# A hybrid trunk kernel whose planner ranks instructions by deadlines and has other durations for some forms

## The chip, the cores and the metric

The kernel runs on one core of a Trainium2 chip. Its time is the device time in microseconds (us). Five instruction streams run side by side: TensorE (PE, matmuls), VectorE (DVE), ScalarE (ACT), GpSimd (POOL) and SyncE (SP, which here only issues DMAs). Each works its own instructions in a fixed order, and waits on semaphores for what another has not yet done.

## What is computed

Two layers of a trunk with three parallel token mixers, on 640 tokens (128 of context and 512 latent ones) of width 1024. All is float32. Cut to its core, one layer is:

```python
shift, scale, gate = split(mod, 3)          # mod = silu(c) @ w_mod + b_mod
h = rms(x, norm_g) * (1 + scale) + shift
proj = h @ w_in                             # all inputs of the branches and gates
o_a = attend(q, k, v)                       # latent attention, softmax over 640 keys
qkv = silu(dwconv(qkv_b, conv_w))           # gated DeltaNet, both directions, 4 heads
Tinv = triangular_solve(A + eye, eye)       # one 64x64 inverse per chunk, head, direction
o_b = rms(o_f + o_bw, gdn_onorm)
o_c = chunk_mlp(cu, cv)                     # gMLP with a 128x128 mixing matrix per group
yb = [o_a * silu(z_a), o_b * silu(z_b), o_c * silu(z_c)] @ w_branch
x = x + gate * (sum(sigmoid(gl) * yb) @ w_o)
```

## The kernel before

Tokens lie along the free dimension in two halves of 320, channels along the 128 partitions. A dense product of one 128-column block with 1024 input rows is three float32r products for each of eight row tiles (`mm3`: high by high, high by low, low by high), 128x320 each, into one PSUM bank; ACT casts a weight tile `raw` to its high part `hi`, and DVE subtracts that to get `lo`. `hh0` to `hh7` and `hl0` to `hl7` are the high and low parts of h.

The order of a layer in the program: modulation and norm, the four DeltaNet heads with the blocks for q, k and v, the chunk MLP and its blocks, the attention with the branches' products and gates in between, the merge, the output product. The inverse of a head (`inverse`, line 1066) goes in small steps between engines: DVE makes 16x16 inverses, PE multiplies 32x32 blocks (`pa`, line 1107; each step 20 matmuls with a `tile_position`, that is on a part of the array), ACT or DVE takes the result out of PSUM, and so on to 64x64. Its tiles are called `iv`, in PSUM `p2`.

Nothing of this is issued where it is written. `Recorder` records every operation with what it reads and writes; `issue` at the end emits them engine by engine, so that all instructions of the trace have the line 371. The order comes from `plan` (line 214): it simulates the five engines with the durations of `cost` (line 155), and each time an engine is free it takes, of the operations whose inputs and buffers are there, the one with the smallest `op.prio`. That number is the operation's place in the program, lowered by an offset (`rec.hp()`, 100000) for operations that free PSUM or feed the next step. Buffers are handed out in the order of the program for each kind (13 of `G`, 8 of `iv`, 5 of `C`, 3 each of `raw`, `hi` and `lo`, two PSUM banks each for the dense `dn`, for `mm` and for `p2`). `best` (line 206) plans once for each of four values of `SLACKS`, time that is added where PE waits for another engine, and keeps the order with the smallest modelled end.

Names of tiles carry two numbers, `iv_728_796`; below the second is left out. In the inverse of the third head, `R_727` is `brs` (lines 1100 to 1102), `iv_728` is `Bm` (lines 1103 to 1105), and `p2_729` is `pa`, the 20 matmuls that read it.

Of the kernel before, what the change touches and what calls it, by code (L numbers as in the profile page):

```python
# [8 lines left out]
F32R = mybir.dt.float32r  # L9
# [39 lines left out]
HOP = {"V": 36, "S": 36, "G": 60, "PE": 53, "SP": 60}  # L49
AFTER = {"V": 33, "S": 122, "G": 60}  # L50
SLACKS = (0, 60, 120, 180)
ISSUE = 475
DMA_LAG, DMA_RATE = 1900, 340.0

# [5 lines left out]
class Recorder:  # L60
# [94 lines left out]
    def cost(self, op, outs, ins):  # L155
        size = lambda x: x.free_size() if callable(x.free_size) else x.free_size
        e = op.eng
        op.ld = 0
        if e == "SP":
            big = max((x.nbytes() if callable(x.nbytes) else x.nbytes) for x in outs + ins)  # L160
            op.occ, op.lat = ISSUE, big / DMA_RATE
        elif e == "PE":
            n = size(outs[0])
            rows, cols = ins[0].ap[0][1], size(ins[0])
            if op.meth == "transpose":
                op.ld, op.occ = 109, n / 2.4 + 2
            elif ins[0].dtype == F32R:
                op.ld, op.occ = 109, n / 2.4 + 13.7
            elif rows <= 32:
                op.ld, op.occ = 15, n  # L170
            elif rows <= 64:
                op.ld, op.occ = 60, 2 * n
            elif cols == 32:
                op.ld, op.occ = 50, 0.43 * n
            elif cols == 64:
                op.ld, op.occ = 80, 1.3 * n
            else:
                op.ld, op.occ = 109, max(4 * n / 2.4 + 6, 222)
            op.lat = op.occ + 180
        else:  # L180
            n = max(size(x) for x in outs[:1] + ins[:1])
            ps = any(self.tag.get(x.tensor.name, ("", False, 0))[1] for x in outs + ins)
            if e == "V":
                quick = op.meth in ("tensor_scalar", "tensor_copy", "memset") and not ps
                d = 165 if n <= 16 else 165 + (0.66 if quick else 1.09) * n
                if n >= 250:
                    d = 150 + (0.63 if quick else 1.145 if n >= 640 and op.meth == "scalar_tensor_tensor" else 1.05) * n
                elif ps and n > 100:
                    d += 40
                if op.meth == "reciprocal":  # L190
                    d = 165 + 5.5 * n
            elif e == "S":
                d = 160 + 0.84 * n + (190 if "accum_out" in op.kw else 0)
                if op.meth == "activation" and n <= 128:
                    d = max(d, 350) + (45 if outs[0].dtype == F32R else 0)
                elif not ps or outs[0].dtype == F32R:
                    d += 45 if n <= 128 or op.meth == "activation" else 25 if n == 640 else 0
                if op.meth == "copy" and not ps and n == 512:
                    d = 620
            else:  # L200
                d = 200 + 1.2 * n
            op.occ, op.lat = d - TAIL[e], d
            if e == "S" and n == 160 and outs[0].ap[0][1] == 32:
                op.occ, op.lat = 260, 320

    def best(self):

        plans = []
        for slack in SLACKS:
            self.plan(slack)  # L210
            plans.append((self.total, slack))
        return self.plan(min(plans)[1])

    def plan(self, slack):
        import heapq
# [1594 lines left out]
```

## Time and profile before

| | |
|---|---|
| median of 3 runs | 1681.33 us (1680.39 to 1683.24) |
| the profiled execution, its own time | 1683.82 us |
| its span, first to last instruction | 1681.9 us |
| PE busy | 1636.5 us, 97% |
| DVE busy | 1284.8 us, 76% |
| ACT busy | 890.2 us, 53% |
| POOL busy | 16.7 us, 1% |
| mean granted clock of PE | 0.989 |

The span is that of one execution under the profiler; 1.9 us of its time lie outside it. Since PE is busy nearly throughout, the time is read as PE's work plus PE's waits: a list of waits says what PE waited for, and a timeline where. DVE and ACT count where PE waits for one of them. Stretches of 40 us show in which part of the program the waits lie: 0 to 60 us is the start, 120 to 320 the DeltaNet heads with the chunk MLP, 320 to 640 the attention, and the second layer repeats it 835 us later.

### The profile page before, as it was taken

The numbers are of one execution on the slowest core, as the hardware profiler recorded it, in microseconds if no ns is written. First come the engines' busy times: TensorE is split into PE (matmuls) and PEld (weight loads), VectorE is DVE, ScalarE is ACT, GpSimd is POOL, SyncE is SP. The second block draws the span as 40 slices with busy tenths as digits, with TensorE's granted clock in tenths as the row PEclk, the third lists the DMA queues.
The fourth block names the chain that finished last, engine by engine and source line by source line (L and its number), as shares of the span: only waits on it lengthen the run. The fifth ranks groups of instructions, "written<-read, shape, count | busy, mean of one in ns | idle before, by whom it ended". The sixth has DMA issues, their size and how long they took to land. (4 is left out here: it accounts for less than half of the span.)

```text
span 1681.9 us, 34993 instructions
## 1 busy us (share of the span) xinstructions
PE 1636.5 (97%) x13286; PEld 1538.7 (91%) x13286; DVE 1284.8 (76%) x3638; ACT 890.2 (53%) x2201; POOL 16.7 (1%) x100
## 2 busy tenths in 40 slices
PE   6999998999999999999999999989999999999998
PEld 5998988999889989989989989989998899899998
DVE  4898898665655768877988987976656557789898
ACT  3566664554545554434445676646545455545453
POOL 0000000000000000000000000000000000000000
PEclk9999999999999999999989999999999999999999
DMA  9312211222121212555542212212211122113342
GB/s 298 95 56 55 62 58 50 66 69 62 46 60 58 91 51 97 178 185 157 188 156 64 58 42 63 58 50 78 70 52 53 49 64 88 57 65 98 94 161 80
DMA packets 94616, 146.39 MB, mean 87 GB/s; under 512 B 14064, under 2 KB 38000, under 8 KB 94448
## 3 DMA queue, kind: packets, MB, share of 16 engines
q1 hardware_dynamic: 94448, 144.15, 28.0%
q8 instruction: 105, 1.72, 0.4%
q14 instruction: 63, 0.52, 0.1%
HBM read 132.28 MB, written 11.83 MB: 86 GB/s over the span
## 5 line engine op out<-in xcount | busy, mean ns | idle before, releaser
L371 PE MATMUL dn<-hh,hi 128*128 128x320 f32 (+1 forms) x1472 | 469.6, 319 | 4.8 <-ACT hh L371 2.1
L371 PE MATMUL dn<-hl,hi 128*128 128x320 f32 (+1 forms) x1472 | 469.1, 319 | 0.4 <-DVE hl L371 0.3
L371 PE MATMUL dn<-hh,lo 128*128 128x320 f32 (+1 forms) x1472 | 467.9, 318 | 0.0
L371 ACT CAST hi<-raw 128x512 fp32r<-128x512 f32 (+1 forms) x300 | 186.1, 620 | 198.5 <-PE dn L371 101.1
L371 PEld LDWEIGHTS dn<-hh,hi 128*128 128x128 f32 (+1 forms) x1472 | 277.1, 188 | 10.1 <-ACT hh L371 3.1
L371 PEld LDWEIGHTS dn<-hl,hi 128*128 128x128 f32 (+1 forms) x1472 | 277.6, 189 | 3.7 <-DVE hl L371 1.2
L371 PEld LDWEIGHTS dn<-hh,lo 128*128 128x128 f32 (+1 forms) x1472 | 277.5, 189 | 2.9 <-issue 1.0
L371 DVE TENSOR_TENSOR lo<-raw,hi 128x512 fp32r<-128x512 f32 (+1 forms) x300 | 206.5, 689 | 60.3 <-ACT hi L371 57.5
L371 PE MATMUL dn<-qkv,hi 128*128 128x320 f32 x768 | 175.0, 313 | 0.5 <-DVE iv L371 0.5
L371 PEld LDWEIGHTS dn<-qkv,hi 128*128 128x128 f32 x768 | 129.4, 189 | 3.3 <-ACT hi L371 1.6
L371 PE MATMUL dn<-qkv,lo 128*128 128x320 f32 x384 | 119.9, 312 | 0.0
L371 ACT CAST hi<-D 128x512 fp32r<-128x512 f32 x88 | 54.6, 623 | 105.9 <-PE dn L371 51.8
L371 PE MATMUL p<-hh,hi 128*128 128x320 f32 x296 | 92.3, 313 | 0.3 <-ACT hi L371 0.3
L371 PE MATMUL p<-hh,lo 128*128 128x320 f32 x296 | 92.2, 312 | 0.0
L371 PE MATMUL p<-hl,hi 128*128 128x320 f32 x296 | 92.0, 311 | 0.2 <-DVE hl L371 0.2
L371 DVE TENSOR_REDUCE mx<-p 128x1 f32<-128x640 f32 x64 | 52.7, 823 | 48.1 <-PE p L371 48.0
L371 ACT ACTIVATE V<-p,mx,scl 128x640 f32<-128x640 f32 x64 | 56.9, 888 | 60.5 <-DVE mx L371 57.2
L371 PEld LDWEIGHTS dn<-qkv,lo 128*128 128x128 f32 x384 | 72.4, 189 | 0.7 <-issue 0.7
L371 PE MATMUL p<-G,hi 128*128 128x320 f32 x286 | 69.3, 308 | 0.0
L371 ACT ACTIVATE th<-dn 128x320 f32<-128x320 f32 x112 | 48.7, 435 | 38.9 <-PE dn L371 38.2
L371 PEld LDWEIGHTS p<-iv,G 32*32 32x32 f32 (+2 forms) x608 | 34.9, 132 | 36.2 <-issue 33.1
L371 PE MATMUL p<-G,G 128*128 128x512 f32 x128 | 65.7, 595 | 0.0
(350 smaller groups left out, 3484.0 us busy)
## 6 DMA issues: line engine op xcount, KB each, us to landing
raw<-in_w_in SPq DMA_DIRECT2D x212, 256.0 KB, 2.7
G<-in_w_mod SPq DMA_DIRECT2D x96, 256.0 KB, 4.4
raw<-in_w_branch SPq DMA_DIRECT2D x48, 256.0 KB, 2.8
D<-in_w_in SPq DMA_DIRECT2D x32, 256.0 KB, 3.3
ld<-sp SPq DMA_DIRECT2D x16, 320.0 KB, 3.1
raw<-in_w_o SPq DMA_DIRECT2D x20, 256.0 KB, 3.1
G<-in_w_uq SPq DMA_DIRECT2D x16, 192.0 KB, 2.7
D<-in_w_o SPq DMA_DIRECT2D x12, 256.0 KB, 3.6
```

The source lines that it names most:

```text
L371: op.ins = getattr(getattr(nc, ENG[op.eng]), op.meth)(*op.args, **op.kw)
```

## The change

`cost` gets other durations for three forms: DVE operations on PSUM with 100 to 250 elements that are no `scalar_tensor_tensor` cost 165 + 0.95 ns an element; a `scalar_tensor_tensor` of 250 to 640 elements costs 30 ns more above 320 elements and 40 ns more with a float32r output; an ACT activation of 250 elements or more whose bias or scale is a tile costs 50 ns more. `deadlines` goes backward through a plan and gives each operation the latest start that does not move the plan's end, from the starts of those that read its result, of those that take over its buffers, and on PE of the matmul behind it. `best` plans for each slack four times: first with the priorities of before, then three times with the latest starts of the plan just made as priorities. It keeps the plan with the smallest modelled end of the sixteen.

```diff
@@ -49,6 +49,7 @@
 HOP = {"V": 36, "S": 36, "G": 60, "PE": 53, "SP": 60}
 AFTER = {"V": 33, "S": 122, "G": 60}
 SLACKS = (0, 60, 120, 180)
+ROUNDS = 4
 ISSUE = 475
 DMA_LAG, DMA_RATE = 1900, 340.0
 
@@ -186,7 +187,9 @@
                 if n >= 250:
                     d = 150 + (0.63 if quick else 1.145 if n >= 640 and op.meth == "scalar_tensor_tensor" else 1.05) * n
                 elif ps and n > 100:
-                    d += 40
+                    d = d + 40 if op.meth == "scalar_tensor_tensor" else 165 + 0.95 * n
+                if op.meth == "scalar_tensor_tensor" and 250 <= n < 640:
+                    d += (30 if n > 320 else 0) + (40 if outs[0].dtype == F32R else 0)
                 if op.meth == "reciprocal":
                     d = 165 + 5.5 * n
             elif e == "S":
@@ -195,6 +198,8 @@
                     d = max(d, 350) + (45 if outs[0].dtype == F32R else 0)
                 elif not ps or outs[0].dtype == F32R:
                     d += 45 if n <= 128 or op.meth == "activation" else 25 if n == 640 else 0
+                if op.meth == "activation" and n >= 250 and "accum_out" not in op.kw and any(isinstance(op.kw.get(x), bass.AP) for x in ("bias", "scale")):
+                    d += 50
                 if op.meth == "copy" and not ps and n == 512:
                     d = 620
             else:
@@ -203,13 +208,47 @@
             if e == "S" and n == 160 and outs[0].ap[0][1] == 32:
                 op.occ, op.lat = 260, 320
 
+    def deadlines(self, out):
+
+        succ = {op.n: [] for op in out}
+        for op in out:
+            for p in op.preds:
+                succ[p].append(op)
+        for op, nm in self.slotdeps:
+            for u in self.users[nm]:
+                succ[u.n].append(op)
+        latest, after = {}, None
+        for op in reversed(out):
+            end = self.total
+            for s_ in succ[op.n]:
+                lag = 53 if s_.eng != op.eng else op.occ - op.lat if op.eng == "PE" else 33
+                end = min(end, latest[s_.n] - lag)
+            t = end - op.lat - (DMA_LAG if op.eng == "SP" else 0)
+            if op.eng == "PE":
+                if after is not None:
+                    t = min(t, latest[after.n] - max(op.occ, op.ld))
+                after = op
+            latest[op.n] = t
+        return latest
+
     def best(self):
 
+
+        first = [op.prio for op in self.ops]
         plans = []
         for slack in SLACKS:
-            self.plan(slack)
-            plans.append((self.total, slack))
-        return self.plan(min(plans)[1])
+            prio = first
+            for n in range(ROUNDS):
+                for op, p in zip(self.ops, prio):
+                    op.prio = p
+                out = self.plan(slack)
+                plans.append((self.total, slack, n, prio))
+                late = self.deadlines(out)
+                prio = [late[op.n] for op in self.ops]
+        _, slack, _, prio = min(plans, key=lambda x: x[:3])
+        for op, p in zip(self.ops, prio):
+            op.prio = p
+        return self.plan(slack)
 
     def plan(self, slack):
         import heapq
```

The instructions are the same. Of PE's 11102 rows 7252 stand at the same place in both orders, of DVE's 3504 rows 1248, of ACT's 2003 rows 1042; half of the rows move by one place or none, the farthest on PE by 101. On PE the moves lie in the first 60 us, around 120 to 280 us and 440 to 620 us and at the same places of the second layer.

Three places are shown. The first is DVE in the inverse of the third head of layer 1; `D_583` to `D_595` are the five scalings of the chunk MLP's norm, `ld_831` frees the PSUM bank `dn_830`, and `G_701` belongs to the fourth head. The rows of before around `iv_728`:

```order
L371 TENSOR_TENSOR br2_694_762<-br__693_761,r_689_757 128x5
L371 TENSOR_TENSOR res_692_760<-res_692_760,br__693_761 128x5
L371 TENSOR_TENSOR G_701_769<-p2_700_768,ir_691_759 128x640
L371 TENSOR_TENSOR iv_728_796<-iv_728_796,R_727_795 128x160
L371 SCALAR_TENSOR_TENSOR ld_831_899<-dn_830_898,lngh_818_886,C_817_885 128x512
L371 TENSOR_SCALAR sg_982_1050<-r_689_757 128x5
L371 TENSOR_TENSOR ya4_599_667<-ya4_599_667,ld_831_899 128x512
L371 TENSOR_TENSOR fz_983_1051<-sg_982_1050 128x5
```

And where it stands after the change:

```order
L410 TENSOR_SCALAR R_727_795<-br2_462_530,c_m01_6_74 128x5
L410 TENSOR_TENSOR R_576_644<-fz_574_642,R_575_643 128x5
L410 SCALAR_TENSOR_TENSOR R_598_666<-R_598_666,R_597_665 128x5
L410 SCALAR_TENSOR_TENSOR R_727_795<-br2_462_530,c_m01_6_74,R_727_795 128x5
L410 SCALAR_TENSOR_TENSOR R_576_644<-R_576_644,R_575_643 128x5
L410 SCALAR_TENSOR_TENSOR R_597_665<-R_598_666,R_597_665 128x5
L410 TENSOR_TENSOR iv_728_796<-iv_728_796,R_727_795 128x160
L410 SCALAR_TENSOR_TENSOR R_575_643<-R_576_644,R_575_643 128x5
L410 TENSOR_TENSOR R_598_666<-R_596_664,R_597_665 128x5
L410 SCALAR_TENSOR_TENSOR D_819_887<-th_827_895,dn_826_894 128x320
```

`R_727` and `iv_728` moved from behind `G_701` to a place ahead of the scalings. The rows that follow the scalings on DVE after the change are these:

```order
L410 TENSOR_SCALAR D_589_657<-D_589_657,mv_580_648,R_597_665 128x512
L410 TENSOR_SCALAR D_592_660<-D_592_660,mv_580_648,R_597_665 128x512
L410 TENSOR_SCALAR D_595_663<-D_595_663,mv_580_648,R_597_665 128x512
L410 SCALAR_TENSOR_TENSOR D_819_887<-th_829_897,dn_828_896 128x320
L410 SCALAR_TENSOR_TENSOR ld_831_899<-dn_830_898,lngh_818_886,C_817_885 128x512
L410 TENSOR_TENSOR ya4_599_667<-ya4_599_667,D_819_887 128x640
L410 TENSOR_TENSOR R_690_758<-ssq_686_754,r_689_757 128x10
L410 TENSOR_TENSOR lo_852_920<-raw_850_918,hi_851_919 128x512
L410 TENSOR_TENSOR iv_725_793<-iv_724_792,p2_731_799 128x5x16 x2
```

`ld_831` now follows the second `D_819`, and a `lo` tile and the next step of the inverse, `iv_725`, follow it.

The second place is PE there. Before:

```order
L371 MATMUL dn_830_898<-C_812_880,D_586_654 128x128
L371 MATMUL dn_830_898<-C_812_880,D_589_657 128x128
L371 MATMUL dn_830_898<-C_812_880,D_592_660 128x128
L371 MATMUL dn_832_900<-C_812_880,D_595_663 128x128
L371 MATMUL p2_729_797<-iv_726_794,iv_728_796 32x32 x20
L371 MATMUL dn_841_909<-hh0_69_137,hi_836_904 128x320
L371 MATMUL dn_841_909<-hl0_70_138,hi_836_904 128x320
L371 MATMUL dn_841_909<-hh0_69_137,lo_837_905 128x320
```

After:

```order
L410 MATMUL dn_830_898<-C_812_880,D_586_654 128x128
L410 MATMUL p2_729_797<-iv_726_794,iv_728_796 32x32 x3
L410 MATMUL dn_830_898<-C_812_880,D_589_657 128x128
L410 MATMUL p2_729_797<-iv_726_794,iv_728_796 32x32 x3
L410 MATMUL dn_830_898<-C_812_880,D_592_660 128x128
L410 MATMUL p2_729_797<-iv_726_794,iv_728_796 32x32 x14
L410 MATMUL dn_832_900<-C_812_880,D_595_663 128x128
L410 MATMUL dn_841_909<-hh0_69_137,hi_836_904 128x320
L410 MATMUL p2_731_799<-iv_724_792,iv_730_798 32x32 x20
L410 MATMUL dn_841_909<-hl0_70_138,hi_836_904 128x320
```

The matmuls `p2_729` moved from behind the last transposition of the chunk MLP (`dn_832`) to between the others, in three pieces, and the next step `p2_731` now follows the first dense matmul of `dn_841`.

The third place is PE in the inverse of the first head; `dn_443` is a dense block. Before:

```order
L371 MATMUL p2_291_359<-iv_287_355,G_216_284 32x32 x20
L371 MATMUL p2_293_361<-iv_280_348,iv_292_360 32x32 x20
L371 MATMUL p2_294_362<-iv_292_360,iv_280_348 32x32 x10
L371 MATMUL dn_443_511<-hh0_69_137,hi_438_506 128x320
L371 MATMUL dn_443_511<-hl0_70_138,hi_438_506 128x320
L371 MATMUL dn_443_511<-hh0_69_137,lo_439_507 128x320
L371 MATMUL dn_443_511<-hh1_76_144,hi_438_506 128x320
```

After:

```order
L410 MATMUL p2_291_359<-iv_287_355,G_216_284 32x32 x20
L410 MATMUL dn_443_511<-hh0_69_137,hi_438_506 128x320
L410 MATMUL dn_443_511<-hl0_70_138,hi_438_506 128x320
L410 MATMUL dn_443_511<-hh0_69_137,lo_439_507 128x320
L410 MATMUL dn_443_511<-hh1_76_144,hi_438_506 128x320
L410 MATMUL dn_443_511<-hl1_77_145,hi_438_506 128x320
L410 MATMUL dn_443_511<-hh1_76_144,lo_439_507 128x320
L410 MATMUL dn_443_511<-hh2_90_158,hi_438_506 128x320
L410 MATMUL p2_293_361<-iv_280_348,iv_292_360 32x32 x20
```

Seven of the dense matmuls moved between two steps of the inverse.

## Rows read from the trace of the kernel before

**Rows 1.** The page's part 1: busy time, share of the span, instructions

```profile
PE 1636.5 (97%) x13286; PEld 1538.7 (91%) x13286; DVE 1284.8 (76%) x3638; ACT 890.2 (53%) x2201; POOL 16.7 (1%) x100
```

**Rows 2.** PE's waits by releaser: us in total, times, longest us

```profile
PE p L371 <- DVE C L371: 12.9, 1, 12.9
PE p L371 <- DVE iv L371: 6.1, 4, 2.7
PE p L371 <- ACT iv L371: 5.9, 4, 2.6
PE p L371 <- DVE R L371: 2.2, 1, 2.2
```

**Rows 3.** Stretches: length, busy us of each engine, PE clock, DMA share, GB/s

```profile
0.00:40.00 40.00, 24.92 (x257) 19.78 (x258) 19.84 (x53) 14.98 (x24) 0.71 (x13) 0.96 0.96 307
240.00:280.00 40.00, 34.53 (x410) 30.40 (x410) 32.21 (x123) 23.23 (x82) 2.77 (x5) 0.96 0.18 56
320.00:640.00 320.00, 319.85 (x2409) 294.71 (x2408) 201.68 (x562) 166.28 (x388) 0.00 (x0) 0.99 0.21 62
```

**Rows 4.** Timeline of PE at place D: start, us, work, idle before

```profile
262.14 0.55 PE L371 MATMUL p<-iv,iv 32*32 32x32 f32 x40 [2.69 <-DVE iv L371]
262.80 0.63 PE L371 MATMUL dn<-hh,hi 128*128 128x320 f32 x1
...
264.43 0.76 PE L371 MATMUL p<-iv,iv 32*32 32x32 f32 x40
```

**Rows 5.** Timeline of DVE at the same place

```profile
255.53 2.37 DVE L371 TENSOR_SCALAR D<-D,mv,R 128x512 f32<-128x512 f32 x5
257.81 0.70 DVE L371 TENSOR_TENSOR lo<-raw,hi 128x512 fp32r<-128x512 f32 x1
258.41 0.50 DVE L371 SCALAR_TENSOR_TENSOR D<-th,dn 128x320 f32<-128x320 f32 x1
...
261.75 0.33 DVE L371 TENSOR_TENSOR iv<-iv,R 128x160 f32<-128x160 f32 x1
261.98 0.76 DVE L371 SCALAR_TENSOR_TENSOR ld<-dn,lngh,C 128x512 f32<-128x512 f32 x1
```

**Rows 6.** Stretches of PE alone: length, busy us, granted clock, DMA share, GB/s

```profile
262.70:266.10 3.40, 3.30 (x49) 0.50 0.02 7
371.90:375.40 3.50, 3.50 (x16) 0.51 0.11 43
863.50:873.70 10.20, 8.10 (x40) 0.50 0.22 83
```

**Rows 7.** Timeline of PE at place A

```profile
144.82 0.84 PE L371 MATMUL p<-iv,iv 32*32 32x32 f32 x60 [2.58 <-ACT iv L371]
```

**Rows 8.** Timeline of DVE at the same place

```profile
145.57 0.69 DVE L371 SCALAR_TENSOR_TENSOR qkv<-C,C 128x512 f32<-128x512 f32 x1 [1.86 <-ACT C L371]
```

**Rows 9.** Timeline of PE at place B

```profile
206.22 0.84 PE L371 MATMUL p<-iv,iv 32*32 32x32 f32 x60 [0.39 <-ACT iv L371]
...
210.09 0.33 PE L371 MATMUL p<-iv,G 64*64 64x64 f32 x2 [0.34 <-DVE iv L371]
```

**Rows 10.** Timeline of PE at place E

```profile
278.38 0.49 PE L371 MATMUL mm<-Q,G 128*128 128x128 f32 x2 [0.46 <-ACT Q L371]
...
279.60 0.42 PE L371 MATMUL dn<-hh,hi 128*128 128x320 f32 x1 [0.47 <-DVE ld L371]
```

**Rows 11.** Timeline of PE around one group of small matmuls

```profile
267.67 0.55 PE L371 MATMUL p<-iv,G 32*32 32x32 f32 x40
268.15 0.42 PE L371 MATMUL dn<-hh,hi 128*128 128x320 f32 x1
268.41 0.31 PE L371 MATMUL dn<-hl,hi 128*128 128x320 f32 x1
268.55 0.31 PE L371 MATMUL dn<-hh,lo 128*128 128x320 f32 x1
```

**Rows 12.** Timeline of PE at the first dense matmul

```profile
26.13 0.35 PE L371 MATMUL dn<-hh,hi 128*48 128x320 f32 x1 [1.75 <-ACT hh L371]
```

## The prediction

> **What bounds the kernel now.** I read the busy shares first: TensorE (PE) works 1636.5 of 1681.9 us [rows 1]. The rest is 45.4 us, so no order of the same instructions can win more than that and the stretches in which PE runs slower than it could. Then the list of PE's waits, to see what those 45 us are: 12.9 us stand before the first matmul, 12.0 us are eight waits for tiles `iv`, the longest of them 2.7 and 2.6 us, and 2.2 us are one wait for `R` [rows 2]. The times of the waits come in pairs 835 us apart, one for each layer; below, a place of the first layer stands for both. Then the stretches: 34.53 us of PE work in 240 to 280 us, 24.92 in the first 40, but 319.85 of 320 in the attention [rows 3]. So the attention has nothing to give, and the inverse of the DeltaNet heads (`iv`) and the two ends have. Last the granted clock: it is 0.50, the lower of the two levels, in short stretches, some behind a wait of PE, some behind none [rows 6].
>
> **The change part by part.** Nothing is removed or added on the chip: the same 11102 PE, 3504 VectorE (DVE), 2003 ScalarE (ACT) and 601 DMA rows stand in the two orders. Only the order changes, and each place is priced by what PE waits for there.
>
> *Place D, the third head's inverse (262 us, and 1097).* PE's 20 small matmuls `p2_729` wait 2.69 us for DVE [rows 4]. Their last input, `iv_728`, is the 0.33 us product that DVE does at 261.75, behind the evacuation `G_701` and a row of small r products [rows 5]. The new order puts it, with the two small `R_727` operations that it needs, ahead of the five `D` scalings (2.37 us), some 8 us earlier. So `p2_729` will not wait; it runs between the `dn_830` matmuls that the scalings pace. Next late is then `ld_831`: it frees the bank for `dn_841`. Today it starts at 261.98 [rows 5]; in the new order it stands right behind the scalings and one `D_819` (0.50). The scalings end at 255.53 + 2.37 = 257.90 today; `iv_728` (0.33) and one `lo` (about 0.6 of its 0.70) now stand ahead of them, some small r products (about 0.3) behind. That gives 258.5 for their end, 259.0 behind `D_819`, 259.8 behind `ld_831` (0.76), and `dn_841` starts at about 259.85 instead of 262.80 [rows 4]: 2.95 us earlier. Part goes back: behind `p2_731` DVE now does `lo_852`, the ya4 sums, a transposition and a product, then ACT copies, before the next small matmuls, and PE has only the 24 `dn_841` matmuls as cover. At one matmul each 0.147 us (268.55 less 268.41 is 0.14; over the longer runs it is 0.147) [rows 11] that is 3.5 us, against a chain of 3.24 us today (264.43 to 267.67) [rows 4, 11] that gains one `lo` or sum of 0.7 [rows 5]. The new wait is between 0 and 1.2 us; I take 0.65. Net -2.3 for each layer, **-4.6**; between -3.5 and -5.9.
>
> *Place A, the first head's inverse (144.8 us, and 980).* `p2_293` waits 2.58 us for ACT behind `p2_291` [rows 7]. Seven `dn_443` matmuls (7 x 0.147 = 1.03 us) now stand between the two, since ACT copies their bank free first. But a 0.69 us convolution product now precedes the last `iv_287` on DVE [rows 8], so the chain starts later by it. 2.58 - 1.03 - 0.69 would be 0.86 if all the delay fell before `p2_291`; some of it shows as a wait there. I take -0.6 for each layer, **-1.2**; between -2.6 and +0.8 (no matmul gained, the product late in full).
>
> *Place B (206 us, and 1042).* Waits of 0.39 and 0.34 us [rows 9]: ACT now copies `iv_503` and `iv_505` ahead of the `G_501`, `G_502` copies. Both go at most; **-1.3** for the two layers, at least -0.4 if only one goes in each.
>
> *Place E (279 us, and 1115).* Waits of 0.46 and 0.47 us [rows 10]; DVE's release of the dense bank moves ahead of two evacuations. About 0.4 for each layer, **-0.8**; between 0 and -1.8.
>
> *Small groups.* A group of 32- or 64-row matmuls in a run of dense ones costs its own work and a step before and behind: 268.15 to 268.41 is 0.26 where the next is 0.14 [rows 11], so 0.11, and about as much before it, 0.2 together. The new order has 264 such groups, the old 244. Eight of the 20 lie in the first 100 us, and I count them with the start; four are the pieces of `p2_729`, between matmuls that wait for DVE anyway, two are at A; six others lie in PE's full stretches. 8 x 0.2 = **+1.6**; between 0 and 4.0. [...]
>
> *Between the layers.* PE waits 2.2 us for `R` [rows 2]. Eight of the modulation matmuls move into the first wait, but three move ahead of the sums that start its chain, and DVE does modulation rows before the first normalised tile. **+0.3**; between -1 and +1.5.
>
> *The start.* x is loaded first, ahead of two small loads, so PE's first work can come a little earlier than at 12.9 us [rows 2]; I count 0.6. But on SP's queue `raw_59`, `raw_62` and `raw_65` go from rows 23, 31 and 33 to rows 45 to 47, behind 20 more modulation loads of 256 KB. At 307 GB/s [rows 3] those 20 are 5.2 MB or 17 us. Before, the 24 matmuls on `raw_62` for the first four rows of x (24 x 0.147 = 3.5 us) filled PE while the modulation loads came in; the new order does them last. From 26.13 us on PE had hardly a gap [rows 12], so a wait that opens behind it is a loss. Two can: for `hh2`, the third row of x, whose modulation is the next to be made, and for the cast of `raw_59`. The nearest row is the wait for the first `hh`, 1.75 us [rows 12]; I take 1.1 for `hh2`, since its modulation loads stand earlier in the queue than before, and 0.5 for the cast. **+1.0**; between -1 and +3.5 (all 24 missing).
>
> *The attention and the last 80 us.* PE had no wait to lose in the attention [rows 3]. What I looked for is cover: between a head's scores and the transposition of its softmax the old order has PE work worth 2.2 us at the least and the new one 2.7, each counted by 0.147 for a dense matmul. 0, between -1 and +2. On PE the last 80 us are the same row for row; DVE's rows move by some sums: 0, between -0.5 and +0.8.
>
> Sum: -4.6 - 1.2 - 1.3 - 0.8 + 1.6 + 0.3 + 1.0 = **-5.0 us**. Against the profiled execution, 1683.8 (its span 1681.9 and 1.9 around it), that is 1678.8. The median of the three runs, 1681.3, is 2.5 below that execution, so the time to forecast is **1676.3 us**.
>
> **The rivals.**
> *The clock comes with it.* Behind the wait at D, PE runs at half clock for 3.4 us [rows 6], which costs half of it, 1.7 us; so it does in the other layer. If the shorter wait lets the clock stay up, it is 1676.3 - 3.4 = 1672.9, and with the stretch at A as well (another 1.7) 1671.2. For it: these stretches follow waits of 2 to 3 us. Against it: one of the same length stands at 371.9 us, behind no wait [rows 6], and PE stays thinly loaded at D while the scalings pace it. [...] Chance 0.25.
>
> *The waits only move.* At D the chain behind `p2_731` and at A the later `iv_287` take the upper bounds (1.2 and all of the gain), and the extra groups cost 4.0: -3.5 + 0 - 0.4 + 4.0 + 0.3 + 1.0 and nothing at E is +1.4; with half of that, about 1681. DVE at 76% in one fixed order makes it possible. Against it: 2.95 us at D are freed by moving a single 0.33 us operation whose inputs are long there. Chance 0.17.
>
> *The start becomes slower than all this gains.* One mechanism: the three late `raw` loads. If PE finds nothing to do where the 24 matmuls on `raw_62` and the first 12 on the other two stood, that is 36 x 0.147 = 5.3 us of waits, and a stretch like the one between the layers, 10.2 us at half clock [rows 6], costs 5.1 more. 10.4 in place of the 1.0 makes 1676.3 + 9.4 = 1685.7. It decides against the kernel from a loss of 6.0 us at the start on. For it: the start is where the queues are full (DMA share 0.96 in the first 40 us [rows 3]). Against it: the total of bytes is the same and the modulation, for which all rows of x wait, comes sooner. Chance 0.12.
>
> *It does not do what it says.* That the ranking by deadlines picks the old order is excluded, since the orders differ. That durations put right for a few forms change nothing on the chip by themselves is true, and priced above.
>
> **How the numbers follow.** The forecast, 1673.5 to 1679.5, has 0.46. A change under 0.2% (3.4 us, about what a measurement here tells from none) is from 1678.0 to 1684.7. Faster: three quarters of 0.46 and the 0.25 of the clock, 0.59; same: the rest of the forecast and nearly all of the 0.17, 0.28; slower 0.13. The range takes in the clock at D and A with some of A's and D's bounds, and on the other side moved waits and a part of the loss at the start: 1669 to 1683.
>
> **What would show it.** D right: `p2_729` without a wait, `dn_841` some 3 us earlier against the matmuls before it, 240 to 280 us with over 36.5 us of PE work. The next wait there names the DVE or ACT tile of the same head. A: two waits of about 0.6 and 1.2 instead of one of 2.58. Start: the first dense matmul near 25.5 to 26.5 us, and PE in 20 to 60 us with 1 to 2 us less work than before. Attention: still no wait. Wrong would be a PE wait above 2 us at D or A, or above 3 us between 26 and 45 us.

## The result

The changed kernel takes 1665.1 us (median of four runs, 1663.0 to 1667.1) against 1682.1 us: a ratio of 0.990, 95% interval 0.9882 to 0.9917. On another chip it took 1660.9 us against 1679.5 us (0.9889, 0.9871 to 0.9908). It is faster, as forecast, but by 17 to 19 us instead of 5, below the range of 1669 to 1683. Two executions that lay far from all others, one of e_D with 2647 us and one of the kernel before with 6139 us, are left out of every figure below.

The profiled execution after has a span of 1661.1 us, 20.8 less than before. Its page, part 1 (answers to [rows 1]):

```profile
PE 1626.3 (98%) x13286; PEld 1529.8 (92%) x13286; DVE 1274.3 (77%) x3638; ACT 885.1 (53%) x2201; POOL 16.6 (1%) x100
```

PE's idle time is the span less its busy time: 45.4 us before and 1661.1 - 1626.3 = 34.8 us after, 10.6 less. The other 10.2 us are the same work of PE in less time, and the clock differs. The list of cores gives span and mean granted clock, first of before, then of after:

```profile
core 0: 1681.9 us, clock 0.989
```

```profile
core 0: 1661.1 us, clock 0.997
```

1681.9 x (1 - 0.989) is 18.5 us, which is about half of the 37.5 us of the eight stretches at half clock in that trace (granted clock 0.50 or 0.51). After, three stretches of 3.4 us are left (0.50), and 1661.1 x 0.003 is 5.0. So **the span times the mean clock is about what the order would take at full clock**: 1663.4 us before, 1656.1 after. By that, 7.3 of the 20.8 us are the order and 13.5 the clock. But it charges the clock with too much. In the stretch at half clock at 147 us before, the dense matmuls start 0.27 us apart, as here, and 0.147 at a clock of 1.00 [rows 11], so 0.45 of the time of the work there is lost and not half:

```profile
147.06 0.47 PE L371 MATMUL dn<-hh,hi 128*128 128x320 f32 x1
147.33 0.47 PE L371 MATMUL dn<-hl,hi 128*128 128x320 f32 x1
147.60 0.47 PE L371 MATMUL dn<-hh,lo 128*128 128x320 f32 x1
```

And it counts PE's waits within a stretch as work. PE works 34.85 us in the eight stretches of before and 9.97 in the three of after; 0.45 of that is 15.7 and 4.5. By this count, which gives the traces without any stretch the same work (1621.3 us in e_again, 1622.1 in e_rounds, described below) as these two (1620.8 and 1621.8), **11.2 of the 20.8 us are the clock and 9.6 the order**: 10.6 of idle time less, 1.0 of work more. The runs without a trace have only their mean clock, so the table below has span times clock; between kernels whose clocks differ as these two do, it is off by some 2 us. The clock is given to 0.001, which is 1.7 us in one run.

PE's waits after, by releaser (us in total, times, longest), answer to [rows 2]:

```profile
PE p L410 <- DVE C L410: 11.6, 1, 11.6
PE dn L410 <- ACT hh L410: 4.5, 3, 2.2
PE p L410 <- DVE G L410: 3.6, 4, 1.6
PE dn L410 <- DVE ld L410: 2.0, 4, 0.8
PE mm L410 <- DVE G L410: 1.9, 6, 0.5
PE mm L410 <- DVE Q L410: 1.5, 2, 0.8
PE mm L410 <- ACT iv L410: 1.2, 1, 1.2
...
PE p L410 <- ACT iv L410: 0.6, 2, 0.3
```

The eight waits for `iv`, 12.0 us before, are two of 0.3. New are two of 1.6 us for a `G` of DVE and one of 1.2 for an `iv` copy. The stretches (length, PE's busy us, clock, DMA share, GB/s), answer to [rows 3] and [rows 6]:

```profile
0.00:40.00 40.00, 26.11 (x265) 0.96 0.93 299
...
240.00:280.00 40.00, 38.66 (x454) 1.00 0.15 45
316.50:319.90 3.40, 3.40 (x26) 0.50 0.27 77
320.00:640.00 320.00, 318.48 (x2354) 1.00 0.21 63
...
855.80:859.20 3.40, 3.17 (x17) 0.50 1.01 373
```

240 to 280 us has 38.66 us of PE work at full clock instead of 34.53. Here is place D on PE, answer to [rows 4] (start, us, work):

```profile
253.89 0.26 PE L410 MATMUL p<-iv,iv 32*32 32x32 f32 x6
254.08 0.49 PE L410 MATMUL dn<-C,D 128*128 128x128 f32 x2
254.50 0.26 PE L410 MATMUL p<-iv,iv 32*32 32x32 f32 x6
254.68 0.49 PE L410 MATMUL dn<-C,D 128*128 128x128 f32 x2
255.10 0.44 PE L410 MATMUL p<-iv,iv 32*32 32x32 f32 x28
255.47 0.49 PE L410 MATMUL dn<-C,D 128*128 128x128 f32 x2
256.01 0.41 PE L410 MATMUL dn<-hh,hi 128*128 128x320 f32 x1
256.36 0.55 PE L410 MATMUL p<-iv,iv 32*32 32x32 f32 x40
```

`p2_729` runs in three pieces among the transpositions, with no wait, and `dn_841` starts 0.05 us behind `ld_831` on DVE (answer to [rows 5]):

```profile
252.39 2.37 DVE L410 TENSOR_SCALAR D<-D,mv,R 128x512 f32<-128x512 f32 x5
254.67 0.48 DVE L410 SCALAR_TENSOR_TENSOR D<-th,dn 128x320 f32<-128x320 f32 x1
255.21 0.75 DVE L410 SCALAR_TENSOR_TENSOR ld<-dn,lngh,C 128x512 f32<-128x512 f32 x1
255.88 0.81 DVE L410 TENSOR_TENSOR ya<-ya,D 128x640 f32<-128x640 f32 x1
...
257.29 0.37 DVE L410 TENSOR_TENSOR iv<-iv,p 128x80 f32<-128x80 f32 x2
```

### The profile page after: what moved, and what is told of

Its sections match the earlier page's. It is cut to its first block, busy times and chain, and to the rows that moved or that the text cites. A ratio compares the mean times of both kernels' runs of the same rounds, so it can differ in the third digit from the quotient of the medians.

```text
span 1661.1 us, 34986 instructions
## 1 busy us (share of the span) xinstructions
PE 1626.3 (98%) x13286; PEld 1529.8 (92%) x13286; DVE 1274.3 (77%) x3638; ACT 885.1 (53%) x2201; POOL 16.6 (1%) x100
## 4 chain that ended last, share of the span: by engine, by line
PE 88%; DVE 6%; ACT 4%; DMA 2%; issue 1%; SPq 0%; DVEq 0%; ACTq 0%
PE dn L410 45%; PE p L410 26%; PE mm L410 17%; DVE C L410 1%; DVE lo L410 1%; ACT G L410 1%; DVE G L410 1%; ACT iv L410 1%; DVE iv L410 1%; ACT hi L410 1%; DMA raw<-in_w_in 1%; DMA G<-in_w_uq 0%; ACT C L410 0%; DVE ya L410 0%; DVE R L410 0%
## 5 line engine op out<-in xcount | busy, mean ns | idle before, releaser
L410 PEld LDWEIGHTS dn<-hh,hi 128*128 128x128 f32 (+1 forms) x1472 | 274.9, 187 | 11.2 <-ACT hh L410 5.3
L410 ACT COPY V<-p 128x640 f32<-128x640 f32 x64 | 44.2, 691 | 52.2 <-PE p L410 51.9
L410 PEld LDWEIGHTS p<-iv,G 32*32 32x32 f32 (+2 forms) x608 | 34.8, 134 | 36.9 <-issue 36.5
```

What stands on the lines that cost most here:

```text
L410: op.ins = getattr(getattr(nc, ENG[op.eng]), op.meth)(*op.args, **op.kw)
```

## The experiments

All times are medians beside runs of the kernel before on the same chip. The last column is the mean over the runs of span times clock. Counted from the traces instead (span less 0.45 of PE's work at half clock), the order at full clock is 1666.2 us before, 1656.6 changed, 1661.7 in e_cost, 1654.7 in e_rounds, 1666.5 in e_D, 1662.7 in e_D2 and 1665.9 in e_A.

| kernel | us | before there | ratio, 95% interval | mean clock | span x clock |
|---|---|---|---|---|---|
| before (23 runs beside e_cost, e_rounds, e_D and e_A) | 1681.6 | | | 0.990 | 1663 |
| changed | 1665.1 | 1682.1 | 0.990, 0.9882 to 0.9917 | 0.9955 | 1656 |
| e_again (changed, again) | 1660.9 | 1679.5 | 0.9889, 0.9871 to 0.9908 | 0.998 | 1655 |
| e_cost | 1676.5 | 1681.6 | 0.9968, 0.9955 to 0.998 | 0.991 | 1660 |
| e_rounds | 1657.7 | 1681.6 | 0.9861, 0.9845 to 0.9877 | 0.9985 | 1654 |
| e_rounds2 (e_rounds, again) | 1662.0 | 1679.5 | 0.9898, 0.9883 to 0.9913 | 0.996 | 1654 |
| e_D | 1679.9 | 1681.6 | 0.9984, 0.9974 to 0.9994 | 0.9915 | 1663 |
| e_D2 | 1674.0 | 1679.5 | 0.9966, 0.9954 to 0.9978 | 0.993 | 1661 |
| e_A | 1679.6 | 1681.6 | 0.9987, 0.9979 to 0.9995 | 0.992 | 1663 |
| e_wait | 1668.6 | 1680.7 | 0.993, 0.9906 to 0.9955 | 0.994 | 1657 |
| e_psum | 1667.0 | 1680.7 | 0.9914, 0.989 to 0.9937 | 0.996 | 1657 |
| e_stt | 1660.4 | 1680.7 | 0.9876, 0.9858 to 0.9894 | 0.999 | 1656 |
| e_act | 1665.2 | 1680.7 | 0.9908, 0.9892 to 0.9924 | 0.9945 | 1654 |
| e_fine2 | 1662.7 | 1679.5 | 0.9892, 0.9867 to 0.9917 | 0.995 | 1652 |

**Which part of the change?** e_cost has the new durations and the old ranking:

```diff
-                    d += 40
+                    d = d + 40 if op.meth == "scalar_tensor_tensor" else 165 + 0.95 * n
+                if op.meth == "scalar_tensor_tensor" and 250 <= n < 640:
+                    d += (30 if n > 320 else 0) + (40 if outs[0].dtype == F32R else 0)
...
+                if op.meth == "activation" and n >= 250 and "accum_out" not in op.kw and any(isinstance(op.kw.get(x), bass.AP) for x in ("bias", "scale")):
+                    d += 50
```

> The new durations alone, with the old ranking. If the ranking by deadlines makes the gain: within 3 us of before (1679 to 1685 us), the waits of 2.6 and 2.7 us at A and D still there. If the durations make it: about 1665 to 1670 us, these waits gone.

It took 1676.5 us, 5 less than before: neither, but a result between the two. Waits of 2.08 us stand at A in both layers, and D has 0.94 and 0.87 in place of 0.56 and 2.69.

e_rounds has the changed kernel's `deadlines` and `best` with the durations of before, the diff above undone.

> The three rounds of ranking alone, with the old durations. If the ranking makes the gain: 1664 to 1669 us, the waits at A and D under 1 us. If the durations make it: 1678 to 1685 us. If both are needed: about half, 1672 to 1676 us.

1657.7 us, below all three: the ranking makes the gain. (Whether it is the latest starts, or only the choice among sixteen plans in place of four, no run here tells apart.) Its profiled execution has no stretch at half clock:

```profile
core 0: 1654.7 us, clock 1.000
```

It even lay 7.5 us below the changed kernel, and my first reading was that the new durations spoil the order. That was to be tested next.

**Do the new durations spoil it?** e_psum, e_stt and e_act are e_rounds with one of the three durations each: the PSUM forms, `scalar_tensor_tensor`, the activations.

> The three rounds with the new duration of the VectorE forms on PSUM alone. If one of the three new durations spoils the order, one of these three kernels comes out near the changed kernel's 1665 us with its waits of 1.6 us near 316 and 1142 us, the other two near 1658 us. If any change of a duration only shuffles the order, all three lie somewhere between 1656 and 1668 us, each with its longest waits at other places.

> The three rounds with the new durations of scalar_tensor_tensor alone; the expectations are those of the PSUM one: near 1665 us with the waits of 1.6 us at 316 and 1142 us if this duration is at fault, near 1658 us if it is not; between 1656 and 1668 us with other waits if every change only shuffles.

> The three rounds with the new duration of the ScalarE activations alone; the expectations are those of the PSUM one: near 1665 us with the waits of 1.6 us at 316 and 1142 us if this duration is at fault, near 1658 us if it is not; between 1656 and 1668 us with other waits if every change only shuffles.

1667.0, 1660.4 and 1665.2 us: no single culprit. e_psum has waits of 1.41 us at 321 and 1147 us, e_stt of 1.3 us at 315 and 1139, e_act none above 1 us there. Each duration gives another order. By span times clock the three lie at 1657, 1656 and 1654 us, far closer than their medians.

So I ran the changed kernel and e_rounds side by side, 5 rounds on one chip.

> The changed kernel again, on the same chip as e_rounds2, for a direct comparison: 1663 to 1667 us; the granted clock of its runs between 0.994 and 0.997, and the span shorter by about 1.3 us for each 0.001 of clock.

> The three rounds with the old durations again: 1656 to 1660 us, 6 to 8 us below the changed kernel, with a clock of 0.997 to 1.000. If the first result was luck of the clock: within 3 us of the changed kernel.

1660.9 and 1662.0 us: no difference, as if the first result was luck of the clock, and my reading fell. The clock had gone the other way round: now it is the changed kernel whose profiled execution has none of the stretches, and e_rounds three. The two lists of cores, e_again first:

```profile
core 0: 1656.0 us, clock 1.000
```

```profile
core 0: 1660.4 us, clock 0.996
```

The instruction order is the same as in the first runs, so the stretches are not fixed by it. The durations, worth 5 us with the old ranking, add nothing on top of the new one. What both chips agree on is span times clock: 1656 and 1655 us for the changed kernel, 1654 and 1654 for e_rounds. Whether these 2 us are real, the resolution of the clock leaves open.

e_fine2 lets the changed kernel choose among ten slacks, `SLACKS = tuple(range(0, 200, 20))`.

> The changed kernel with ten slacks from 0 to 180 in place of four; it keeps slack 80 and the third ranking. If more plans to choose from give a better order: 1657 to 1662 us. If the plans that the model likes best differ on the chip by chance: 1660 to 1669 us, that is no better than the changed kernel.

1662.7 us with a clock of 0.995: not told from the changed kernel by its time.

**Place D alone.** e_D sorts the order of before once more, with these operations moved in both layers (8660 is the distance between the layers in recorded operations). The first row puts `R_727` and `iv_728` ahead of the scalings, the row left out the 20 matmuls `p2_729` ahead of `dn_832`, the last `ld_831` ahead of `lo_852`:

```diff
+MOVES = (
+    ((2838, 2840), 2234, -0.5, (0, 8660)),
...
+    ((3184,), 3259, -0.5, (0, 8660)),
+)
...
+        key = {op.n: float(i) for i, op in enumerate(out)}
+        for ns, mark, side, layers in MOVES:
+            for layer in layers:
+                for i, n in enumerate(ns):
+                    key[layer + n] = key[layer + mark] + side + 0.001 * i
+        out = sorted(out, key=lambda op: key[op.n])
```

> The order of before with place D alone moved, in both layers: R_727 and iv_728 ahead of the scalings, p2_729 ahead of the last transposition, ld_831 up. Wait and clock belong together: 2.3 us less of waits a layer and no half-clock stretch behind D, 1.5 us more, so 7 to 8 us in all, about 1674.5 us. The clock goes its own way: 4.6 us less, about 1677.5 us, with a stretch at half clock still within 20 us of D. The wait only moves: within 1 us of before.

1679.9 us, 1.7 less: for the most part the wait only moved. PE's timeline at D in e_D, the rows with the last wait:

```profile
256.70 0.49 PE L386 MATMUL dn<-C,D 128*128 128x128 f32 x2 [0.48 <-DVE D L386]
257.36 0.41 PE L386 MATMUL dn<-hh,hi 128*128 128x320 f32 x1 [0.17 <-DVE ld L386]
...
263.00 0.55 PE L386 MATMUL p<-iv,G 32*32 32x32 f32 x40 [2.05 <-DVE iv L386]
263.49 0.62 PE L386 MATMUL dn<-hh,hi 128*128 128x320 f32 x1
```

The 2.69 us are gone, and two steps later `p2_736` waits 2.05. DVE shows why: the next step of the inverse is ready for it at 258.8, when `p2_731` ends, but stands in its order behind `G_701` and the sums, at 261.50:

```profile
258.29 0.55 PE L386 MATMUL p<-iv,iv 32*32 32x32 f32 x40
```

```profile
259.30 0.82 DVE L386 TENSOR_TENSOR G<-p,ir 128x640 f32<-128x640 f32 x1
260.04 0.17 DVE L386 TENSOR_SCALAR sg<-r 128x5 f32<-128x5 f32 x1
260.10 0.69 DVE L386 TENSOR_TENSOR ya<-ya,ld 128x512 f32<-128x512 f32 x1
...
261.50 0.38 DVE L386 TENSOR_TENSOR iv<-iv,p 128x80 f32<-128x80 f32 x2
```

In the changed kernel that `iv` operation stands at 257.29, right behind one `lo`. e_D2 adds to e_D thirteen operations put behind the inverse's next three:

```diff
+    ((2746, 2747, 2750, 2751, 2748, 2749, 2752, 2753, 3700, 3185, 3701, 3187, 3188), 2885, 0.5, (0, 8660)),
```

> The order of before with place D moved as in e_D, and besides, on DVE in both layers, thirteen other operations put behind the next three of the inverse (iv_725, iv_732). If e_D's new wait of 2.05 us was DVE's order alone, it goes: waits of at most 0.7 us at D, the half-clock stretches there gone, 5 us less of waits and 3 us of clock than before, 1673 to 1676 us. If each wait removed only uncovers the next, another one of 1.5 to 2 us opens within 10 us behind it: 1678 to 1680 us.

1674.0 us, 5.5 less than before there. D has no wait above 0.5 us, and its stretches at half clock are gone (length, PE's busy us, clock):

```profile
145.30:148.70 3.40, 3.40 (x13) 0.50 0.00 0
255.00:268.00 13.00, 12.11 (x243) 1.00 0.24 69
1085.00:1100.00 15.00, 14.09 (x255) 1.00 0.18 59
```

The stretch at A, which e_D2 leaves as it was, is still there (first row), as is that at 974.7. So the gain of D needs two places of DVE's order, not the one that I priced.

**Place A alone.** e_A moves, on ACT, `iv_292` and the two operations that free the dense bank ahead of three `iv_290` and two `G` copies, and a weight's cast and `lo` behind them: `((1127, 1629, 1665), 1100, -0.5, (0, 8660)), ((2240, 2241), 1665, 0.5, (0, 8660))`.

> The order of before with place A alone moved, on ACT in both layers: iv_292 and the two operations that free the dense bank (C_422, C_424) ahead of three iv_290 and two G copies, a weight cast behind them. Wait and clock belong together: 2.0 us less of waits a layer, and the half-clock stretches behind A (1.9 and 3.5 us of loss) gone, about 9 us in all, 1673 us. The clock goes its own way: 4 us less, 1678 us, with the stretches elsewhere. The wait only moves, as my prediction had it for the most part: 1 to 2 us less, 1680.5 us.

1679.6 us, 1.9 less. Again the wait moved on; PE in e_A:

```profile
142.59 0.84 PE L385 MATMUL p<-iv,iv 32*32 32x32 f32 x60 [0.42 <-ACT iv L385]
...
147.53 0.29 PE L385 MATMUL p<-iv,G 64*64 64x64 f32 x2 [1.68 <-DVE iv L385]
```

2.58 became 0.42, and 1.68 opened further on in the same inverse. But from 141 to 151 us the clock is 1.00: the stretch of before at 146.7 is gone, and so is that at 979.5. That is one execution; over the twelve runs the mean clock is only 0.002 above that of before, where these two stretches are worth 0.003.

**Wait and clock.** e_wait puts waits back into the changed kernel at A: on ACT five `G` copies and a cast ahead of `iv_292` in layer 1, three `G` copies in layer 2.

> The changed kernel's order, but on ACT five G copies and a weight cast stand ahead of iv_292 in layer 1, and three G copies in layer 2, so that p2_293 waits again: about 2.5 us at 144 us, 1.3 us at 970 us. Wait and clock belong together: a half-clock stretch of 3.4 us behind the longer wait (1.7 us more) and none behind the shorter one; 2.2 + 1.0 + 1.7 is 4.9 us slower than the changed kernel, about 1670 us. The clock goes its own way: no stretch between 144 and 152 us, 3 us slower, about 1668 us.

The waits came out at 2.63 and 1.44 us:

```profile
144.97 1.19 PE L424 MATMUL p<-iv,iv 32*32 32x32 f32 x60 [2.63 <-ACT iv L424]
...
975.93 0.84 PE L424 MATMUL p<-iv,iv 32*32 32x32 f32 x60 [1.44 <-ACT iv L424]
```

and the clock of the two places (length, PE's busy us, clock):

```profile
143.90:150.70 6.80, 5.73 (x85) 0.50 0.11 36
974.50:981.30 6.80, 5.37 (x110) 1.00 0.18 54
```

The longer wait came with a half-clock stretch of 6.8 us, twice what I expected, which began 1.1 us before the wait ended; the shorter had none. In this execution wait and clock belong together there. The time, 1668.6 us, is between the two expectations and can't decide, since the clock of the four runs lay between 0.990 and 0.998.

Over the fourteen traces, outside the start and the change of layers: of eleven waits of 2.5 us and more, eleven had such a stretch, which began between 1.1 us before their end and 1.9 us behind it; of four of 2.05 to 2.08 us, three; of fifteen of 1.2 to 1.7 us, two. The eleven are two places only, A and D, in five of the traces. At the change of layers it holds less: of eleven waits of 2.15 to 2.28 us there, four.

## Why the prediction was wrong

The sum was for the order alone, -5.0 us. By the runs the order gave 1663 - 1656 = 7, and 8 on the other chip; by the two traces, 9.6. **The step that failed is the clock**: the forecast priced it at nothing, and the rival *The clock comes with it* had 0.25 and at most 5.1 us. In the two traces the clock gave 11.2 of the 20.8 us. By the mean clock of the runs the kernel before loses 1680 x 0.010 = 17 us to it, the changed one 1663 x 0.0045 = 7.5 on the first chip and 4 on the second: so 9 us on the one and, from 14.5 before, 10.7 on the other; this way of counting has up to a fifth too much. Either way it is about half of the change. Without it the time would have been some 8 to 11 us longer, inside the range. I had counted only the stretches behind D and one at A. The trace of before has more of them: 6.8 us at 979.5, the 10.2 us between the layers [rows 6], of which after has 3.4, those at 371.9 and 1208.2, and one at the start, which stays. Against the rival I had held that PE stays thinly loaded at D; after the change the clock from 240 to 280 us is 1.00. And the mean clock of 0.989 was in view: it is worth 18.5 us by one multiplication. The other half of the miss is the order's own sum, which was too small by 2 to 5 us, above all at A.

Point by point, PE's waits in the two profiled executions, before and after:

- **D**, -2.3 a layer: 0.56 + 2.69 became 0.06, -3.2. The mechanism was right, and the term came out a little beyond the bound of 2.95 a layer, in part by the 0.56 that I had not priced: I took 0.65 for a new wait at `p2_736`, and none came, since DVE does the next `iv` right behind one `lo`. Had only what I priced moved, e_D shows the term: 0.48 + 0.17 + 2.05 of 3.25 left, -0.55.
- **A**, -0.6 a layer: 2.58 + 0.24 became 0.29, -2.5 (2.58 became 0.29 in layer 2), and 0.49 opened 8 us behind. This was the term most under-sized: two layers are past its bound of -2.6. I charged the 0.69 us product [rows 8] against the last `iv_287`. In the trace after, that `iv` operation starts at 140.88, where it stood at 140.96, though the places before it run 0.55 us later: a 0.89 us convolution step that stood between had moved ahead of it. And the four `iv_290` copies end at 143.21 in place of 144.45.
- **B**, -0.65 a layer: 0.39 + 0.34 became one wait of 0.18. Right.
- **E**, -0.4 a layer: 0.46 + 0.47, and 0.52 at 292 us, became 0.26 + 0.82 + 0.29, -0.1. The dense bank is still waited for.
- **The start**, +1.0: the third row of x does wait, 0.78 us (forecast 1.1), but the first matmul came 1.3 us sooner (forecast 0.6). The same matmuls near 118 us start 0.5 us later than before, although the waits ahead of them are 1.2 us shorter: PE's work there takes some 1.7 us longer. That would fit the eight extra small groups, but was not measured apart. The start was no rival: nothing near 9 us.
- **Between the layers**, +0.3: 2.17 + 0.55 + 0.32 of waits became 0.53 + 2.21, -0.3. The wait moved from the chain's transpositions to the first `hh`.
- **The fourth head and the attention**, 0: wrong by 4.4. 1.62 us opened at 316 us and again at 1142, in the fourth head's inverse, and 1.17 at 378, where ACT's cast had itself waited 2.49 us for a load (`in_cache_ckvT`). I had looked for cover under the softmax, and no wait above 0.4 us came there; I had not looked at the fourth head. There DVE does a `D` that waits for ACT ahead of the `G` that PE needs, the last row:

```profile
316.10 0.29 PE L410 MATMUL p<-iv,G 64*64 64x64 f32 x2 [1.62 <-DVE G L410]
```

```profile
313.85 0.55 DVE L410 SCALAR_TENSOR_TENSOR D<-dn,l_q_a_norm,D 128x320 fp32r<-128x320 f32 x1 [2.06 <-ACT D L410]
314.31 0.63 DVE L410 TENSOR_SCALAR G<-p 32x160 f32<-32x160 f32 x2
...
315.29 0.66 DVE L410 TENSOR_SCALAR G<-p 32x160 f32<-32x160 f32 x2
```

- **The last 80 us**, 0: waits of 0.52 and 0.89 became one of 0.23, -1.2, on DVE's order alone.
- **Small groups**, +1.6: not measured apart. PE's work less 0.45 of its time at half clock grew by 1.0, but over the fourteen traces this work lies anywhere between 1619.5 and 1623.8 us.

*The waits only move* was a true mechanism: e_D and e_A show it for each place moved alone. It did not hold for the change, which moved the following steps as well.

## What to carry to other kernels

Multiply the span by one less the mean granted clock before anything else: here this was the price of the stretches at half clock, a little too high (18.5 us, against 15.7 counted from PE's work in them), and it exceeded the waits that I worked on (12.0 for all eight waits for `iv`). In these queues, worked in order, moving the operation that PE waits for bought little by itself (1.7 and 1.9 us for waits of 5.4 and 5.2): a later step of the same chain came to wait (2.05 us in e_D, 1.68 in e_A), and the ranking had to move the whole chain. Compare orders as close as these on one chip, side by side, and by span times clock beside their times: the 7.5 us (0.45%) between the changed kernel and e_rounds became 1.1 us the other way side by side.

## What the runs showed of the hardware

One order did not have one clock. The changed kernel's eight runs lay between 0.994 and 1.000, and its profiled executions have three stretches at a granted clock of 0.50 on one chip and none on the other, with the same long waits to within 0.25 us. What sets where a stretch falls, no run here shows.

Stretches also followed work in which PE waited for nothing above 0.4 us in the 20 us ahead of them: eleven, at 364 to 372 and 1190 to 1208 us in seven of the traces, all within 2.5 us behind the end of 20 matmuls of one column each (`mm<-c_ones,qkv`), in which PE counts as busy. Before, around 370 us (length, PE's busy us, clock):

```profile
369.40:371.80 2.40, 2.40 (x23) 1.00 0.76 236
371.90:375.40 3.50, 3.50 (x16) 0.51 0.11 43
```

So a stretch began here behind rows without idle time. The 20 matmuls run twice in each of the fourteen traces, and behind seventeen of the 28 no stretch followed, the changed kernel's four among them; why not was not tried, and that these matmuls are the cause is not shown.
